# Own buffer for the pool weights, pool products ordered behind the sigmoid, two adding transfers in the output projection, and a bank of its own for the last half tile

## The chip, the cores and the metric

The kernel runs on one core of a Trainium2 chip. The metric is device time in microseconds (us) of one execution; lower is better. Engines are named as in the profile: PE is TensorE, DVE is VectorE, ACT is ScalarE, POOL is GpSimd, SP is SyncE, which here only issues transfers. Transfers are issued from a queue of SP, ACT or POOL.

## The reference

One decoder block for S = 512 tokens of width D = 1024, in float32. h = RMSNorm(x) is projected to q, k, v, a pool input u and two gates per output column. Differential attention in 8 heads and a multi-scale causal pool are gated, added, projected and added to x; a squared-ReLU MLP of width 4096 and a last norm follow.

```python
u_q, u_k, u_v, u_pool, u_gate = jnp.split(rmsnorm(x, g1) @ w_in, splits, axis=-1)
a = diff_attention(q, k, v, ...)         # per head: w = softmax_1 - lam * softmax_2, causal; o = w @ v, normed
p = multiscale_pool(u_pool, w_pool, pool_scale)   # per group g: d = windowed mean - u;  y = (d @ w_pool[g]) * scale
gates = jax.nn.sigmoid(u_gate)           # two gates per column
merged = gates[0] * a + gates[1] * p
x = x + merged @ w_out
x = x + relu(rmsnorm(x, g2) @ w_up) ** 2 @ w_down
return rmsnorm(x, gf)
```

There are 4 pool groups; group g serves heads 2g and 2g+1.

## The kernel before

Every product of float32 numbers is computed as three matmuls. A number is split into a high part of reduced precision (`fp32r`) and a low part, the rest; hi·hi, hi·lo and lo·hi are added up in PSUM. Names ending in `h` and `l` (`xh`, `xl`, `wh_`, `wl_`, `vh`, `vl`, `dh`, `dl`) are such parts; `wr_` is the raw weight as it was loaded.

A weight's parts are made in one of two ways. `split_w` casts the raw weight on ACT (L108) and subtracts on POOL, or on the engine that is passed, DVE (L109). With `"dma"`, `get_w` writes the high part on ACT (L116), writes its negative into the low part on ACT (L117), and lets a transfer issued on POOL add the weight out of memory a second time (L118).

The stages follow each other in this order. Up to about 55 us the kernel norms x and computes v for all heads. Up to about 305 us it works through heads 0 to 7: q and k of the head after, scores s, exp, p = the difference of the two softmaxes (L376), transposes t of p on PE (L380), their split (L382, L383), the product with v (PV, L388), and a norm over the head's output o. Between the heads stand 20 fillers, five for each pool group g: the projection and pooling of u (`pool`), and the gate projections ga and gp of its two heads (`gate`, L444). Behind the fifth, one sigmoid on ACT (L477) works on all four gates of the group, a table load (L478) follows, and `merge` runs for the two heads: the product pp of the pooled d and `w_pool` (L455 to L457), its eviction times the gate (L458), the sum with the head's gated output (L459), and its split (L460, L461). From about 305 to 360 us stands the output projection `po`, in two halves of columns, each with four weight blocks kk. Then come four quarters of the MLP, whose products are combined so that fewer are needed, up to 686 us, and the tail: the last product (L715) in three blocks of columns, their adds to x1 (L719), and the last norm and the stores (`square`, `finish`).

The program text is not the order of the work. A scheduler puts each engine's instructions into an order by its own estimate of when each can start, and every engine then works strictly in that order, waiting by semaphores where an operand or a buffer is not ready. `after(later, earlier)` tells this scheduler that one instruction has to come later than another, and creates no semaphore. Buffers are handed out by tag: a new tile of a tag waits until the readers of the tile that had the buffer are done. PSUM has eight banks; in the heads, `acc` gives bank 0, 1 and 2 in turn to the projections and to pp, in the order of the program text. So gp5, pp4, pp5, u3 and ga6 get banks 1, 2, 0, 1 and 2, and po0_0, which starts the output projection's banks over, gets bank 0, the one of pp6.

The pool weights `wpr` (L435) share a tag with other temporaries of the heads. They are cast and subtracted (L438, L439) into the third column of `wt_all`, which the transposes' parts use too.

Of the kernel before, what the change touches and what calls it, by code (L numbers as in the profile page):

```python
# [11 lines left out]
F32 = mybir.dt.float32  # L12
# [3 lines left out]
ALU = mybir.AluOpType  # L16
AX = mybir.AxisListType

P = 128
# [3 lines left out]
H = 8  # L23
NT = S // P
EPS = 1e-6
NCON = 313
LAM_INIT = 0.8 - 0.6 * math.exp(-0.3 * 0)
WINDOWS = (2, 4, 8, 16)
NEG = -3.0e38
# [23 lines left out]
def block_kernel(ctx, tc, xT, x_tok, gains, pos, consts, w_in, w_v, w_pool, w_out, w_up, w_dn, out):  # L53
    nc = tc.nc
    V, A, G, T = nc.vector, nc.scalar, nc.gpsimd, nc.tensor
# [3 lines left out]
    def after(later, earlier):  # L59
        tc.add_manual_dep(  # L60
            later.ins, earlier.ins.name,
            mybir.DependencyInfo(mybir.DependencyClass.NoSync, mybir.DependencyReason.DATA), reason="issue order",
        )

    ctx1 = ExitStack()
    cp = ctx.enter_context(tc.tile_pool(name="cp", bufs=1))
# [21 lines left out]
    def tmp(tag, name, shape=(P, S), dt=F32, bufs=2):  # L88
        return tp.tile(list(shape), dt, tag=tag, name=name, bufs=bufs)
# [22 lines left out]
    def get_w(src, name, eng=None):  # L112
        raw, hi, lo = load_w(src, name)
        if eng == "dma":

            A.copy(out=hi, in_=raw)  # L116
            A.mul(out=lo, in_=f(hi), mul=-1.0)  # L117
            G.dma_start(out=lo, in_=src, accum_op=ALU.add)  # L118
        else:
            split_w(raw, hi, lo, eng=eng)  # L120
        return hi, lo

    def mm3(acc, hi, lo, rh, rl):
# [7 lines left out]
            T.matmul(acc, lhsT=lo[:, c], rhs=rh[:, k, :], start=False, stop=k == NK - 1)  # L131


    con = cp.tile([P, NCON], F32, name="con")
    g1c, g2c, gfc, pscc = (con[:, 8 * i : 8 * i + 8] for i in range(4))
    wv0 = load_w(w_v[0, 0], "v0_0", 2, slice(0, 1))
    nc.sync.dma_start(out=g1c, in_=consts[:, 0:8])
    invc = con[:, 32:40]
    rcc = con[:, 40:56]
    lamv = con[:, 56:312].rearrange("p (a d) -> p a d", a=4)  # L140
    subc = con[:, 312:313]
    posi = cf.tile([P, NT], I32, name="posi")
    xh = B16(0, F32R, "xh")
    xl = B16(1, F32R, "xl")
# [11 lines left out]
        out=mask[:, 384:512], in_=mask[:, 384:512], pattern=[[-1, P]],  # L156
# [42 lines left out]
    for n in range(2):  # L199
        accs = [bank(4 * n + t, f"v{n}_{t}") for t in range(NT)]  # L200
        for kk in range(4):
            if n == 0:
                xprep(2 * kk)
            if n == 0 and kk == 0:
                raw, hi, lo = wv0
                nc.sync.dma_start(out=raw[:, 512:], in_=w_v[0, 0, :, 512:])
            else:
                raw, hi, lo = load_w(w_v[n, kk], f"v{n}_{kk}", 2 if n == 0 else 1)
            for k2 in range(2):
                if n == 0 and k2 == 1:  # L210
                    xprep(2 * kk + 1)
                sl = slice(k2 * 512, k2 * 512 + 512)
# [20 lines left out]
        for t in range(NT):  # L233
# [4 lines left out]
                out=vd[2], in0=av, scalar=rcol[:, t, 0:1], in1=vd[1],  # L238
                op0=ALU.mult, op1=ALU.subtract,
            )  # L240

    nc.sync.dma_start(out=con[:, 8:], in_=consts[:, 8:])
    nc.sync.dma_start(out=posi, in_=pos)

    lpr = tmp("pb", "lpr", (P, 2, 64), bufs=1)
# [13 lines left out]
    r_ = cf.tile(sh, F32, name="r_")  # L259
# [3 lines left out]
        out=r_, in0=posf.rearrange("p (t o) -> p t o", o=1).to_broadcast(sh),  # L263
        in1=invc.rearrange("p (o f) -> p o f", o=1).to_broadcast(sh), op=ALU.mult,
# [45 lines left out]
    acc = Rot((0, 1, 2))  # L310
# [98 lines left out]
    def pool(g):  # L409
        w = WINDOWS[g]  # L410
        a_ = proj(24 + g, f"u{g}", "dma")
        pad = tmp("u", f"u{g}", (P, 16 + S), bufs=1)
        G.memset(pad[:, :16], 0.0)
        u = pad[:, 16:]
        V.tensor_tensor(out=u, in0=a_, in1=rb, op=ALU.mult)
        bufs_ = [tmp("pa", f"pa{g}", (P, 16 + S), bufs=1), tmp("pb", f"pb{g}", (P, 16 + S), bufs=1)]
        for b_ in bufs_[:g]:
            G.memset(b_[:, :16], 0.0)
        cur, s_ = pad, 1
        n = 0  # L420
        while s_ < w:
            nxt = bufs_[n % 2]
            G.tensor_tensor(out=nxt[:, 16:], in0=cur[:, 16:], in1=cur[:, 16 - s_ : 16 + S - s_], op=ALU.add)
            cur, s_, n = nxt, 2 * s_, n + 1
        win = cur[:, 16:]
        d = bufs_[n % 2][:, 16:]
        V.scalar_tensor_tensor(out=d, in0=win, scalar=1.0 / w, in1=u, op0=ALU.mult, op1=ALU.subtract)
        V.tensor_tensor(out=d[:, :w], in0=win[:, :w], in1=rcc[:, :w], op=ALU.mult)
        V.tensor_tensor(out=d[:, :w], in0=d[:, :w], in1=u[:, :w], op=ALU.subtract)
        dh = tmp("dh", f"dh{g}", dt=F32R, bufs=1)  # L430
        dl = tmp("dl", f"dl{g}", dt=F32R, bufs=1)
        A.copy(out=dh, in_=d)
        V.tensor_tensor(out=dl, in0=d, in1=f(dh), op=ALU.subtract)
        wr = tmp("sq", f"wpr{g}", (P, 256))
        nc.sync.dma_start(out=wr, in_=w_pool[:, g, :])  # L435
        wph = wt_all[:, 0, 2, 0:256]
        wpl = wt_all[:, 1, 2, 0:256]
        A.copy(out=wph, in_=wr)  # L438
        V.tensor_tensor(out=wpl, in0=wr, in1=f(wph), op=ALU.subtract)  # L439
        return dh, dl, wph, wpl  # L440
# [2 lines left out]
        a_ = proj(m, name, "dma")  # L443
        V.tensor_tensor(out=dst, in0=a_, in1=rb, op=ALU.mult)  # L444

    def merge(h, a, sa, sp, dh, dl, wph, wpl):
        a, y = a
        if y is not None:
            V.scalar_tensor_tensor(out=a, in0=a, scalar=subc, in1=sa, op0=ALU.mult, op1=ALU.mult)
            V.tensor_tensor(out=a, in0=a, in1=y, op=ALU.mult)  # L450
        else:
            G.tensor_tensor(out=a, in0=a, in1=sa, op=ALU.mult)
        p_ = acc(f"pp{h}")
        c = slice((h % 2) * P, (h % 2) * P + P)
        T.matmul(p_, lhsT=wph[:, c], rhs=dh, start=True, stop=False)  # L455
        T.matmul(p_, lhsT=wph[:, c], rhs=dl, start=False, stop=False)
        T.matmul(p_, lhsT=wpl[:, c], rhs=dh, start=False, stop=True)  # L457
        V.scalar_tensor_tensor(out=sp, in0=p_, scalar=pscc[:, h : h + 1], in1=sp, op0=ALU.mult, op1=ALU.mult)  # L458
        V.tensor_tensor(out=a, in0=a, in1=sp, op=ALU.add)  # L459
        A.copy(out=mh[:, h, :], in_=a)  # L460
        V.tensor_tensor(out=ml[:, h, :], in0=a, in1=f(mh)[:, h, :], op=ALU.subtract)  # L461

    state = {}

    def filler_list():
        for g in range(4):
            def p_(g=g):
                state["gt", g] = tmp("g", f"g{g}", (P, 4, S), bufs=1)
                state["p", g] = pool(g)
            yield p_  # L470
            for i in range(4):
                h = 2 * g + i // 2
                def g_(g=g, i=i, h=h):
                    gate((28, 36)[i % 2] + h, ("ga", "gp")[i % 2] + str(h), state["gt", g][:, i])
                    if i == 3:
                        gt = state["gt", g]
                        sg = A.activation(out=gt, in_=gt, func=AF.Sigmoid)  # L477
                        after(A.preload_act_table_set(EXPLN), sg)  # L478
                yield g_

    fillers = list(filler_list())
    nf = 0
    outs = {}
    cur = qk(0)
    for h in range(H):
        outs[h] = attn(h, *cur)
        cur = qk(h + 1) if h < H - 1 else None
        while nf < LAG[h]:
            fillers[nf]()
            nf += 1  # L490
            if nf % 5 == 0:
                g = nf // 5 - 1
                gt = state["gt", g]
                for i in range(2):
                    merge(2 * g + i, outs[2 * g + i], gt[:, 2 * i], gt[:, 2 * i + 1], *state["p", g])

    ctx1.close()
    bk = ctx.enter_context(tc.tile_pool(name="bk", bufs=1, reuse_waits="tile"))
    acc = Rot(tuple(range(8)))

    x1 = big.tile([P, NT, D], F32, tag="s0", name="x1")
# [42 lines left out]

    po = [acc(f"po0_{t}") for t in range(NT)]
    for kk in range(4):
        w = get_w(w_out[0, kk], f"o0_{kk}", V if kk % 2 else None)
        for k in (2 * kk, 2 * kk + 1):
            for t in range(NT):
                mm_rows(po[t], t, k, w, k == 0, k == NK - 1)  # L550
# [7 lines left out]
    for t in range(NT):  # L558
        a_ = acc(f"po1_{t}")
# [60 lines left out]
    def down(q):  # L620
# [49 lines left out]
        w = parts(x_, "t3", V)  # L670
# [30 lines left out]
        if not last:  # L701
            to_x1(product(A22, w4, "m4", onto=m7), 1, 0)
            return
        for t in (0, 1):
            square(t, 1, yr[:, 1])
        fin = [finish(t, 1) for t in (0, 1)]

        cols = ((0, 0, 512), (1, 0, 256), (1, 256, 512))
        for a, c0, c1 in cols:
            for p in range(4):  # L710
                hi, lo = w4[p // 2]
                sl, tsl = slice((p % 2) * 512 + c0, (p % 2) * 512 + c1), slice(a * P, a * P + P)
                zh, zl = zfh[:, A22, p, tsl], zfl[:, A22, p, tsl]
                for l_, r_ in ((zh, hi), (zh, lo), (zl, hi)):
                    T.matmul(m7[a][:, c0:c1], lhsT=l_, rhs=r_[:, sl], start=False, stop=p == 3 and r_ is hi and l_ is zl,  # L715
                             skip_group_check=True)
            t = 2 + a
            xs = x1[:, t, c0:c1]
            evict = V.tensor_tensor(out=xs, in0=m7[a][:, c0:c1], in1=xs, op=ALU.add)  # L719
            if a == 0:  # L720
                for i in fin:
                    after(i, evict)

            to = 6 if c1 == 256 else 0
            A.activation(out=yr[:, a, c0:c1], in_=xs, func=AF.Square, accum_out=st[:, t, to : to + 1])
            if c1 == 256:
                V.tensor_tensor(out=st[:, t, 1:2], in0=st[:, t, 1:2], in1=st[:, t, 6:7], op=ALU.add)
                row_early(t, 1)
            else:
                finish(t, 0, a == 1)  # L730
# [72 lines left out]
```

## Time and profile before

| | |
|---|---|
| runs | 697.95, 695.3, 697.5 us; median 697.5 |
| the profiled execution | 697.38 us, its span 695.6 us |
| PE busy | 679.3 us, 98% of the span |
| DVE, ACT, POOL busy | 476.4, 420.0, 161.2 us |
| DMA | 100.88 MB, 145 GB/s in the mean |

The profile is one execution. Its span runs from the first instruction to the last; the time of the execution holds 1.8 us more. A row of the timeline gives the start, the duration, the engine, the line, the operation, output and inputs; the bracket behind it tells how long the engine stood idle before, and what it waited for last. "SPq" and "POOLq" are the queues of transfers.

### The profile page before, as it was taken

To read this page: it belongs to the slowest core of one execution; us is meant where nothing else is said; L and a number is where in the kernel's file an instruction comes from. 1 tells how busy PE (TensorE), PEld (TensorE's weight loads), DVE (VectorE), ACT (ScalarE), POOL (GpSimd) and SP (SyncE) were. 2 spreads that over 40 slices of the span, in tenths; PEclk is the share of its full clock that TensorE was granted. 3 is DMA by queue.
4 is the path that set the end of the run, shared out by engine and by line. 5 is a ranking of instruction groups with operands and counts; after the bars stand their busy time and mean duration, and the time that the engine had idled before them with its cause. 6 is when DMAs were issued, how large, how long until landed. Compare 5 with 4: busy or idle time off the path is not lost.

```text
span 695.6 us, 8855 instructions
## 1 busy us (share of the span) xinstructions
PE 679.3 (98%) x3158; PEld 564.3 (81%) x3158; DVE 476.4 (68%) x834; ACT 420.0 (60%) x683; POOL 161.2 (23%) x151
## 2 busy tenths in 40 slices
PE   8999999999999999999999999999999999999995
PEld 7788878888888887787888888888888888888884
DVE  6953977789788875965385675555765567645785
ACT  7554487977986689674356644455434554355544
POOL 6101634264345525532300010000210011000100
PEclk9999999999999999999999999999999999999998
DMA  7534574426436365345943269823797249952523
GB/s 268 165 115 116 133 150 120 103 63 157 125 88 151 99 152 121 91 163 201 246 128 118 91 107 288 231 100 91 179 247 209 90 92 209 248 177 91 95 57 122
DMA packets 30140, 100.88 MB, mean 145 GB/s; under 512 B 3600, under 2 KB 4240, under 8 KB 30096
## 3 DMA queue, kind: packets, MB, share of 16 engines
q1 hardware_dynamic: 22464, 72.79, 30.0%
q0 software_dynamic: 7488, 27.27, 23.0%
q8 instruction: 25, 0.41, 0.2%
q10 hardware_dynamic: 144, 0.26, 0.1%
q14 instruction: 19, 0.16, 0.1%
HBM read 98.20 MB, written 2.10 MB: 144 GB/s over the span
## 4 chain that ended last, share of the span: by engine, by line
PE 78%; DVE 10%; ACT 6%; issue 2%; DMA 2%; POOL 1%; SPq 0%; DVEq 0%; ACTq 0%; POOLq 0%
PE pu L127 8%; PE pu L128 8%; PE pu L131 8%; PE m L652 7%; PE m L653 7%; PE m L651 7%; PE po L536 2%; PE po L537 2%; PE po L538 2%; DVE p L376 2%; PE q L127 2%; PE k L127 2%; PE k L128 2%; PE q L128 2%; PE q L131 2%
## 5 line engine op out<-in xcount | busy, mean ns | idle before, releaser
L127 PE MATMUL pu<-x1gh,wh_up 128*128 128x512 f32 (+1 forms) x272 | 101.0, 377 | 0.2 <-ACT x1gh L571 0.2
L128 PE MATMUL pu<-x1gl,wh_up 128*128 128x512 f32 (+1 forms) x272 | 101.1, 377 | 0.0
L641 POOL DMA_DIRECT2D wr_b<-w_dn x32 | 27.7, 927 | 299.7 <-DVE wl_t L109 228.5
L109 DVE TENSOR_TENSOR wl_up<-wr_up,wh_up 128x1024 fp32r<-128x1024 f32 x32 | 39.2, 1225 | 41.8 <-ACT wh_up L108 30.3
L131 PE MATMUL pu<-x1gh,wl_up 128*128 128x512 f32 (+1 forms) x272 | 64.0, 377 | 0.0
L108 ACT CAST wh_up<-wr_up 128x1024 fp32r<-128x1024 f32 x32 | 33.7, 1053 | 44.4 <-PE m L653 20.0
L127 PEld LDWEIGHTS pu<-x1gh,wh_up 128*128 128x128 f32 x272 | 51.0, 188 | 9.8 <-ACT x1gh L571 0.5
L128 PEld LDWEIGHTS pu<-x1gl,wh_up 128*128 128x128 f32 x272 | 51.2, 188 | 9.6 <-DVE x1gl L572 0.2
L131 PEld LDWEIGHTS pu<-x1gh,wl_up 128*128 128x128 f32 x272 | 49.2, 188 | 9.3
L108 ACT CAST wh_t<-wr_b 128x1024 fp32r<-128x1024 f32 x32 | 33.6, 1053 | 38.1 <-PE m L653 24.6
L109 DVE TENSOR_TENSOR wl_t<-wr_b,wh_t 128x1024 fp32r<-128x1024 f32 x32 | 38.9, 1224 | 22.8 <-ACT wh_t L108 13.2
L604 DVE TENSOR_TENSOR zfl<-zr,zfh 128x512 fp32r<-128x512 f32 (+1 forms) x32 | 34.9, 1091 | 26.8 <-ACT zfh L603 26.8
L651 PE MATMUL m<-wh_t,zfh 128*128 128x512 f32 x120 | 46.7, 389 | 0.0
L652 PE MATMUL m<-wl_t,zfh 128*128 128x512 f32 x120 | 46.7, 389 | 0.0
L653 PE MATMUL m<-wh_t,zfl 128*128 128x512 f32 x120 | 46.7, 389 | 0.0
L371 ACT ACTIVATE p<-p,st 128x128 f32<-128x128 f32 (+3 forms) x64 | 35.8, 560 | 17.6 <-DVE st L367 17.1
L603 ACT CAST zfh<-zr 128x512 fp32r<-128x512 f32 (+1 forms) x32 | 30.2, 944 | 23.6 <-DVE zr L601 16.6
L652 PE MATMUL m<-wl_b,zfh 128*128 128x512 f32 x96 | 37.3, 389 | 0.0
L653 PE MATMUL m<-wh_b,zfl 128*128 128x512 f32 x96 | 37.3, 389 | 0.0
L651 PE MATMUL m<-wh_b,zfh 128*128 128x512 f32 x96 | 37.2, 389 | 0.0
L376 DVE SCALAR_TENSOR_TENSOR p<-p,st 128x128 f32<-128x128 f32 (+3 forms) x32 | 28.9, 902 | 8.0 <-ACT p L375 8.0
L109 DVE TENSOR_TENSOR wl_b<-wr_b,wh_b 128x1024 fp32r<-128x1024 f32 x16 | 19.6, 1224 | 18.4 <-PE pu L131 9.9
(266 smaller groups left out, 1794.4 us busy)
## 6 DMA issues: line engine op xcount, KB each, us to landing
wr_b<-w_dn SPq DMA_DIRECT2D x32, 512.0 KB, 3.8
wr_up<-w_up SPq DMA_DIRECT2D x32, 512.0 KB, 6.2
wr_b<-w_dn POOLq DMA_DIRECT2D x32, 512.0 KB, 5.9
wr_q<-w_in SPq DMA_DIRECT2D x8, 512.0 KB, 3.2
wr_k<-w_in SPq DMA_DIRECT2D x8, 512.0 KB, 3.3
wr_ga<-w_in SPq DMA_DIRECT2D x8, 512.0 KB, 3.2
wr_gp<-w_in SPq DMA_DIRECT2D x8, 512.0 KB, 3.4
wl_ga<-w_in POOLq DMA_DIRECT2D x8, 512.0 KB, 5.7
```

Source lines behind the costliest of these rows:

```text
L108: ins = A.copy(out=hi[:, sl], in_=raw[:, sl])
L109: (eng or G).tensor_tensor(out=lo[:, sl], in0=raw[:, sl], in1=f(hi)[:, sl], op=ALU.subtract)
L127: T.matmul(acc, lhsT=hi[:, c], rhs=rh[:, k, :], start=k == 0, stop=False)
L128: T.matmul(acc, lhsT=hi[:, c], rhs=rl[:, k, :], start=False, stop=False)
L131: T.matmul(acc, lhsT=lo[:, c], rhs=rh[:, k, :], start=False, stop=k == NK - 1)
L371: A.activation(out=pr[:, c, :N], in_=pr[:, c, :N], func=AF.Exp, scale=-1.0, bias=st[:, c : c + 1], accum_out=st[:, 2 + c : 3 + c])
L376: V.scalar_tensor_tensor(out=pr[:, 0, :N], in0=pr[:, 0, :N], scalar=st[:, 4:5], in1=pr[:, 1, :N], op0=ALU.mult, op1=ALU.add)
L603: A.copy(out=zfh[:, sl, p, :], in_=F[:, sl])
L604: V.tensor_tensor(out=zfl[:, sl, p, :], in0=F[:, sl], in1=f(zfh)[:, sl, p, :], op=ALU.subtract)
L651: T.matmul(pa[a], lhsT=zh, rhs=hi[:, sl], start=p == 0 and onto is None, stop=False, skip_group_check=True)
L652: T.matmul(pa[a], lhsT=zh, rhs=lo[:, sl], start=False, stop=False, skip_group_check=True)
L653: T.matmul(pa[a], lhsT=zl, rhs=hi[:, sl], start=False, stop=p == 3 and stop, skip_group_check=True)
```

## The change

1. The constants tile `con` is cut to 57 columns. The four lambda vectors get a temporary tile with its own transfer, so there is one more transfer in the opening.
2. `wpr` gets a buffer of its own. Its load, its cast and its subtraction may so come before other temporaries are done.
3. For heads 4 to 7 the first product of `merge` is ordered after its group's sigmoid.
4. Blocks 0 and 2 of the first half of `w_out` are split by `"dma"`: no POOL subtraction, but one more pass on ACT and an adding transfer each. Blocks 1 and 3 stay on DVE, and the second half is unchanged.
5. In the tail, the last block of columns (256 to 511 of the fourth token tile) is computed in a bank of its own, `m4b`. The sum that lay in its old bank is added to x1 beforehand, by one more DVE instruction, and the second and third block are ordered behind the one ahead of each.

```diff
-    con = cp.tile([P, NCON], F32, name="con")
+    con = cp.tile([P, 57], F32, name="con")
...
-    nc.sync.dma_start(out=con[:, 8:], in_=consts[:, 8:])
+    lamv = tmp("pa", "lamv", (P, 4, 64), bufs=1)
+    nc.sync.dma_start(out=con[:, 8:], in_=consts[:, 8:57])
+    nc.sync.dma_start(out=lamv.rearrange("p a d -> p (a d)"), in_=consts[:, 57:])
...
-        wr = tmp("sq", f"wpr{g}", (P, 256))
+        wr = tmp("wpr", f"wpr{g}", (P, 256), bufs=1)
...
-    def merge(h, a, sa, sp, dh, dl, wph, wpl):
+    def merge(h, sg, a, sa, sp, dh, dl, wph, wpl):
...
-        T.matmul(p_, lhsT=wph[:, c], rhs=dh, start=True, stop=False)
+        first_ = T.matmul(p_, lhsT=wph[:, c], rhs=dh, start=True, stop=False)
+        if h > 3:
+            after(first_, sg)
...
-        w = get_w(w_out[0, kk], f"o0_{kk}", V if kk % 2 else None)
+        w = get_w(w_out[0, kk], f"o0_{kk}", V if kk % 2 else "dma")
...
+        xs = x1[:, 3, 256:512]
+        V.tensor_tensor(out=xs, in0=xs, in1=m7[1][:, 256:], op=ALU.add)
...
         for a, c0, c1 in cols:
+            a_ = acc("m4b")[:, :256] if c0 else m7[a][:, c0:c1]
...
-                    T.matmul(m7[a][:, c0:c1], lhsT=l_, rhs=r_[:, sl], start=False, stop=p == 3 and r_ is hi and l_ is zl,
+                    m = T.matmul(a_, lhsT=l_, rhs=r_[:, sl], start=c0 > 0 and p == 0 and l_ is zh and r_ is hi, stop=p == 3 and r_ is hi and l_ is zl,
                              skip_group_check=True)
+                    if a and p == 0 and l_ is zh and r_ is hi:
+                        after(m, end)
+            end = m
...
-            evict = V.tensor_tensor(out=xs, in0=m7[a][:, c0:c1], in1=xs, op=ALU.add)
+            evict = V.tensor_tensor(out=xs, in0=a_, in1=xs, op=ALU.add)
```

Lines behind these edits move by a few: L455 to L457 become L455, L458 and L459, the eviction L458 becomes L460, and the products L536 to L538 of po become L539 to L541.

The order changes at three places. On PE, around the pool products of heads 4 and 5 (the row of `ss5` is a piece of a head's norm, `t6_2` are transposes of head 6), before:

```order
L401 MATMUL ss5_2239<-sql5_2235,onesr_88 128x512
L131 MATMUL gp5_2611<-xh_81,wl_gp5_2607 128x512
L455 MATMUL pp4_2640<-dh2_2091,wt_531 128x512
L456 MATMUL pp4_2640<-dl2_2092,wt_531 128x512
L457 MATMUL pp4_2640<-dh2_2091,wt_531 128x512
L455 MATMUL pp5_2649<-dh2_2091,wt_531 128x512
L456 MATMUL pp5_2649<-dl2_2092,wt_531 128x512
L457 MATMUL pp5_2649<-dh2_2091,wt_531 128x512
L380 MATMUL t6_2_2458<-ident_83,p6_2_2442 128x128 x3
L127 MATMUL u3_2781<-xh_81,wh_u3_2776 128x512
```

and after:

```order
L401 MATMUL ss5_2241<-sql5_2237,onesr_88 128x512
L130 MATMUL gp5_2613<-xh_81,wl_gp5_2609 128x512
L380 MATMUL t6_2_2460<-ident_83,p6_2_2444 128x128 x3
L126 MATMUL u3_2783<-xh_81,wh_u3_2778 128x512
L455 MATMUL pp4_2642<-dh2_2093,wt_533 128x512
L458 MATMUL pp4_2642<-dl2_2094,wt_533 128x512
L459 MATMUL pp4_2642<-dh2_2093,wt_533 128x512
L455 MATMUL pp5_2651<-dh2_2093,wt_533 128x512
L458 MATMUL pp5_2651<-dl2_2094,wt_533 128x512
L459 MATMUL pp5_2651<-dh2_2093,wt_533 128x512
L127 MATMUL u3_2783<-xl_82,wh_u3_2778 128x512
```

pp4 and pp5 have moved behind the transposes and the first product of u3.

On PE in the first half of the output projection (`vh` and `vl` stand for the merged, split rows), around the pool products of heads 6 and 7, before:

```order
L537 MATMUL po0_3_2994<-wl_o0_2_3058,vh_107 128x512
L538 MATMUL po0_3_2994<-wh_o0_2_3057,vl_108 128x512
L400 MATMUL ss7_2764<-sqh7_2758,onesr_88 128x512
L401 MATMUL ss7_2764<-sql7_2760,onesr_88 128x512
L455 MATMUL pp6_2963<-dh3_2820,wt_531 128x512
L456 MATMUL pp6_2963<-dl3_2821,wt_531 128x512
L455 MATMUL pp7_2973<-dh3_2820,wt_531 128x512
L456 MATMUL pp7_2973<-dl3_2821,wt_531 128x512
L457 MATMUL pp6_2963<-dh3_2820,wt_531 128x512
L457 MATMUL pp7_2973<-dh3_2820,wt_531 128x512
L536 MATMUL po0_0_2991<-wh_o0_0_2997,vh_107 128x512
```

After, they stand between two rows of po0_3 and po0_2:

```order
L539 MATMUL po0_3_2996<-wh_o0_1_3030,vh_107 128x512
L540 MATMUL po0_3_2996<-wl_o0_1_3031,vh_107 128x512
L455 MATMUL pp6_2965<-dh3_2822,wt_533 128x512
L458 MATMUL pp6_2965<-dl3_2823,wt_533 128x512
L459 MATMUL pp6_2965<-dh3_2822,wt_533 128x512
L455 MATMUL pp7_2975<-dh3_2822,wt_533 128x512
L458 MATMUL pp7_2975<-dl3_2823,wt_533 128x512
L459 MATMUL pp7_2975<-dh3_2822,wt_533 128x512
L539 MATMUL po0_2_2995<-wh_o0_0_2999,vh_107 128x512
L540 MATMUL po0_2_2995<-wl_o0_0_3000,vh_107 128x512
L541 MATMUL po0_2_2995<-wh_o0_0_2999,vl_108 128x512
L539 MATMUL po0_2_2995<-wh_o0_0_2999,vh_107 128x512
```

and further on come the first reader of `wl_o0_2`, the norm of head 7 and the first product of po0_0:

```order
L541 MATMUL po0_2_2995<-wh_o0_1_3030,vl_108 128x512
L541 MATMUL po0_3_2996<-wh_o0_1_3030,vl_108 128x512
L539 MATMUL po0_2_2995<-wh_o0_2_3060,vh_107 128x512
L540 MATMUL po0_2_2995<-wl_o0_2_3061,vh_107 128x512
L541 MATMUL po0_2_2995<-wh_o0_2_3060,vl_108 128x512
L539 MATMUL po0_3_2996<-wh_o0_2_3060,vh_107 128x512
L400 MATMUL ss7_2766<-sqh7_2760,onesr_88 128x512
L540 MATMUL po0_3_2996<-wl_o0_2_3061,vh_107 128x512
L541 MATMUL po0_3_2996<-wh_o0_2_3060,vl_108 128x512
L539 MATMUL po0_2_2995<-wh_o0_2_3060,vh_107 128x512
L539 MATMUL po0_0_2993<-wh_o0_0_2999,vh_107 128x512
```

The pool products stand earlier, and between pp7 and po0_0 there are now products of po0_2 and po0_3.

On POOL, around block 0 of `w_out` (L423 are steps of the pooling, L452 a gating product, L397 and L398 pieces of a norm), before:

```order
L118 DMA wl_gp7_2930<-w_in 128x1024
L423 TENSOR_TENSOR pb3_2810<-pa3_2809 128x512
L109 TENSOR_TENSOR wl_o0_0_2998<-wr_o0_0_2995,wh_o0_0_2997 128x1024
L452 TENSOR_TENSOR o5_2231<-o5_2231,g2_2045 128x512
L397 TENSOR_TENSOR sqo6_2505<-o6_2500 128x512
L398 TENSOR_TENSOR sql6_2504<-sqo6_2505,sqh6_2502 128x512
L109 TENSOR_TENSOR wl_o0_2_3058<-wr_o0_2_3055,wh_o0_2_3057 128x1024
```

and after:

```order
L117 DMA wl_gp7_2932<-w_in 128x1024
L423 TENSOR_TENSOR pb3_2812<-pa3_2811 128x512
L452 TENSOR_TENSOR o5_2233<-o5_2233,g2_2047 128x512
L117 DMA wl_o0_0_3000<-w_out 128x1024
L397 TENSOR_TENSOR sqo6_2507<-o6_2502 128x512
L398 TENSOR_TENSOR sql6_2506<-sqo6_2507,sqh6_2504 128x512
L117 DMA wl_o0_2_3061<-w_out 128x1024
L452 TENSOR_TENSOR o6_2502<-o6_2502,g3_2775 128x512
```

The two subtractions are gone; the transfer for block 0 is issued behind the gating product of head 5, the one for block 2 ahead of that of head 6.

More of the change, by code (lines that the diff above doesn't have):

```diff
@@ L25 @@
 EPS = 1e-6
-NCON = 313
 LAM_INIT = 0.8 - 0.6 * math.exp(-0.3 * 0)
@@ L139, in block_kernel @@
     rcc = con[:, 40:56]
-    lamv = con[:, 56:312].rearrange("p (a d) -> p a d", a=4)
-    subc = con[:, 312:313]
+    subc = con[:, 56:57]
     posi = cf.tile([P, NT], I32, name="posi")
@@ L478, in g_ @@
                         after(A.preload_act_table_set(EXPLN), sg)
+                        state["sg", g] = sg
                 yield g_
@@ L494, in block_kernel @@
                 for i in range(2):
-                    merge(2 * g + i, outs[2 * g + i], gt[:, 2 * i], gt[:, 2 * i + 1], *state["p", g])
+                    merge(2 * g + i, state["sg", g], outs[2 * g + i], gt[:, 2 * i], gt[:, 2 * i + 1], *state["p", g])
     ctx1.close()
@@ L777 @@
         + [np.broadcast_to(v.astype(np.float32), (P, v.size)) for v in (
-            inv, np.float32(1) / np.arange(1, 17, dtype=np.float32), lam4.reshape(-1))]
-        + [col(a(subln_g)[0])], axis=1)
+            inv, np.float32(1) / np.arange(1, 17, dtype=np.float32))]
+        + [col(a(subln_g)[0]), np.broadcast_to(lam4.reshape(-1), (P, lam4.size))], axis=1)
     arrays = {
```

## The prediction

> **What bounds the kernel now.** I read the page first, then PE's waits, then busy time in windows, then the timeline around each wait.
>
> ```profile
> span 695.6 us, 8855 instructions
> PE 679.3 (98%) x3158; PEld 564.3 (81%) x3158; DVE 476.4 (68%) x834; ACT 420.0 (60%) x683; POOL 161.2 (23%) x151
> ```
>
> TensorE is busy for 679.3 of 695.6 us, and the change neither adds nor removes a product. So only the 16.3 us in which PE stands can be won, and a new stall costs its full length. The view of PE's waits (engine, line, what it waited for: us, times, longest) names what it stands for:
>
> ```profile
> PE v L217 <- ACT xh L175: 1.9, 1, 1.9
> PE ga L127 <- DVE g L458: 1.4, 1, 1.4
> PE t L380 <- DVE p L376: 1.2, 1, 1.2
> PE m L715 <- DVE x L719: 1.1, 1, 1.1
> PE pp L455 <- ACT wt L438: 1.1, 1, 1.1
> PE po L536 <- DVE g L458: 0.6, 1, 0.6
> ```
>
> The first is in the opening, which keeps its products. The other five are single events and belong to the places that the change touches. The windows (stretch, length, busy time by engine, PE clock, DMA share, GB/s) say whether time won there reaches the end:
>
> ```profile
> 300.00:320.00 20.00, 18.30 (x85) 14.63 (x84) 10.08 (x16) 13.15 (x17) 3.70 (x2) 1.00 0.53 191
> 320.00:340.00 20.00, 20.00 (x90) 16.55 (x89) 11.38 (x22) 9.11 (x15) 8.87 (x6) 1.00 0.80 246
> 400.00:680.00 280.00, 280.00 (x1237) 231.86 (x1236) 178.61 (x221) 138.55 (x164) 24.16 (x28) 1.00 0.60 156
> ```
>
> From 320 us on PE does not stand again until the tail, and the granted clock is 1.00: a microsecond won before 320 us should arrive whole at the end.
>
> **Part 1, pool products behind the sigmoid (pp4, pp5).**
>
> ```profile
> 266.42 0.39 PE L131 MATMUL gp<-xh,wl_gp 128*128 128x512 f32 x1
> 266.65 0.40 PE L455 MATMUL pp<-dh,wt 128*128 128x512 f32 x1
> 267.37 0.68 DVE L444 TENSOR_TENSOR g<-gp,rb 128x512 f32<-128x512 f32 x1
> 268.29 0.48 PE L127 MATMUL u<-xh,wh_u 128*128 128x512 f32 x1
> 272.04 1.28 ACT L477 ACT_TABLE_LOAD   x1
> 273.34 1.92 ACT L477 ACTIVATE g<-g 128x2048 f32<-128x2048 f32 x1
> 275.29 1.41 DVE L458 SCALAR_TENSOR_TENSOR g<-pp,con,g 128x512 f32<-128x512 f32 x2 [3.03 <-ACT g L477]
> 276.09 0.50 PE L127 MATMUL ga<-xh,wh_ga 128*128 128x512 f32 x1 [1.35 <-DVE g L458]
> 276.56 0.48 ACT L382 CAST wt<-t 128x384 fp32r<-128x384 f32 x1
> ```
>
> ga6 takes the bank of pp4, which the eviction L458 frees, which waits for the sigmoid: that is the 1.35 us. The edit orders instructions and adds no semaphore. In the new order pp4 and pp5 move behind three transposes and one product of u, still far ahead of where the sigmoid starts, so the sigmoid still sets ga's start. u3 shares its bank with gp5. Before, six pool products, from 266.65 on at 0.23 each, hid gp5's eviction, which ends at 268.05. After, PE reaches u about 267.0 and stands some 1.1 us: a new wait, on the same L444. It delays PE ahead of the old wait, which shrinks by as much; the two together come to the old 1.35. On ACT the cast of t_2 (0.48), which stood behind the table load, now stands ahead of it. ACT runs without a gap up to 272.04, so sigmoid and ga come 0.48 us later. Cost 0.5. Bounds: were ga's wait gone and only u's left, 1.35 - 1.1 = a gain of 0.25; were both full, with the cast, a cost of 1.1 + 0.48 = 1.6. I take 0.5, since the rows give all its terms.
>
> **Part 2, low parts by adding transfers (blocks 0 and 2 of w_out's first half).**
>
> ```profile
> 283.15 4.23 DVE L376 SCALAR_TENSOR_TENSOR p<-p,st 128x128 f32<-128x128 f32 x1
> 283.30 1.59 POOL L423 TENSOR_TENSOR pb<-pa 128x512 f32<-128x512 f32 x1
> 284.55 2.67 POOL L109 TENSOR_TENSOR wl_o<-wr_o,wh_o 128x1024 fp32r<-128x1024 f32 x1
> 287.52 0.30 PE L380 MATMUL t<-ident,p 128*128 128x128 f32 x1 [1.25 <-DVE p L376]
> ```
>
> A 128x128 operation on DVE lasts 4.23 us, and ends just as POOL's two instructions do: DVE is held for as long as POOL works. By the Trainium skill, "SBUF — State Buffer", section "SBUF: two separate sides", VectorE and GpSimd share a port pair as an exclusive lock; this row fits it. With POOL's subtraction gone, DVE should be free when L423 ends at 284.89, and p is written well before 286.27, where PE began to stand. The gain is 1.25; bounds 0 (another POOL instruction takes its place) and 1.25. I take 1.2.
>
> What replaces it: a pass on ACT and an adding transfer from POOL's queue, for each of two weights. The same pair exists for ga:
>
> ```profile
> 301.23 1.05 ACT L108 CAST wh_o<-wr_o 128x1024 fp32r<-128x1024 f32 x1
> L117 ACT ACTIVATE wl_ga<-wh_ga x8: 1042/1060/1072, 70.2 to 271.0; 128x1024 fp32r<-128x1024 f32 x8
> L118 POOL DMA_DIRECT2D wl_ga<-w_in x8: 858/877/887, 71.5 to 272.3; - x8
> DMA to landing us min/median/max: 5.3/5.6/7.3
> DMA to landing us min/median/max: 8.0/11.9/15.1
> 305.51 0.39 PE L536 MATMUL po<-wh_o,vh 128*128 128x512 f32 x1
> ```
>
> (The first landing row is for L118; the second is for the four POOL loads of w_down at 332 us, the most crowded of this kernel.) For block 2 the cast ends at 302.3, one more cast and the new pass (1.06) end about 304.0, so the transfer lands at 309.3 to 311.3. On PE its first reader stands 43 matmuls behind the start of po (90 in the 20.00 us from 320 on, 0.22 each; with two changes of shape I take 9.0): 305.5 + 9.0 - 0.7 won by then = 313.8. Covered by 2.5 us. If x_tok's four loads, issued at 305.7, stretched it to 11.9, it would land at 315.9 and stall PE 2.1; to 15.1, at 319.1 and 5.3. I take 0.2. Block 0 is cast some 20 us before use. The two ACT passes (2.1 us) fall where ACT has gaps (13.15 of 20 us from 300 on); were they on the path, the cost would be 2.1.
>
> Against this edit speaks the same page of the Trainium skill, section "A bandwidth-pool intuition that's wrong (but worth ruling out)": a DMA issued by GpSimd takes 620 ns alone and 3100 ns while VectorE holds that port, since its descriptors can't be written. This trace shows no such spread: L118's eight issues for ga differ by 29 ns. By the rule the transfer would land 2.5 us later (an estimate from that page), 313.8 at worst, and the sum would be the same by either.
>
> **Part 3, own buffer for the pool weights, and pp6, pp7.**
>
> ```profile
> 309.24 0.68 SPq L435 DMA_DIRECT2D wpr<-w_pool  x1
> 316.90 0.40 ACT L438 CAST wt<-wpr 128x256 fp32r<-128x256 f32 x1 [4.84 <-DMA wpr<-w_pool]
> 317.36 0.50 PE L455 MATMUL pp<-dh,wt 128*128 128x512 f32 x1 [1.09 <-ACT wt L438]
> 318.82 1.41 DVE L458 SCALAR_TENSOR_TENSOR g<-pp,con,g 128x512 f32<-128x512 f32 x2 [1.06 <-PE pp L457]
> 319.63 0.50 PE L536 MATMUL po<-wh_o,vh 128*128 128x512 f32 x1 [0.61 <-DVE g L458]
> ```
>
> The last pool weights are loaded late behind x_tok, land after 7.6 us, and PE waits 1.09 for their cast; then po_0 waits 0.61 for pp6's eviction, whose bank it takes. After, load and cast are done some 40 us earlier, and 21 products (4.8 us) stand between pp7 and po_0 against an eviction of 1.41. Both go: 1.70. Bounds 0 (the wait turns into block 2's) and 1.70; I take 1.7, the transfer's own risk being counted above. The earlier loads, casts (0.40) and subtractions keep their number; the split second constants load adds one issue in the opening, behind work of v, at nothing; were that cover gone, 0.7 for the issue.
>
> **Part 4, the tail.**
>
> ```profile
> 686.41 0.42 DVE L719 TENSOR_TENSOR x<-m,x 128x256 f32<-128x256 f32 x1
> 686.88 0.39 PE L715 MATMUL m<-wh_t,zfh 128*128 128x256 f32 x1 [1.14 <-DVE x L719]
> 688.30 0.28 PE L715 MATMUL m<-wh_t,zfl 128*128 128x256 f32 x1
> 688.62 0.42 DVE L719 TENSOR_TENSOR x<-m,x 128x256 f32<-128x256 f32 x1
> 690.93 0.72 ACT L742 ACTIVATE x<-x,st 128x512 f32<-128x512 f32 x1 [0.48 <-DVE st L530]
> ```
>
> The last twelve products wait 1.14 for the eviction of the other half of their bank. In a bank of their own they do not, and PE ends 1.1 to 1.4 us sooner. But then the last add stands ahead of the third tile's norm chain, which DVE and ACT did during that wait; it costs the end a 0.74 us scaling and parts of 0.2. Gain 0.75; bounds 0.3 and 1.2. The new add (0.42 by the same rows) comes about 669 us, where PE is saturated: nothing, or 0.42 if DVE were late with weights.
>
> **Sum** against the profiled execution (697.38 us; its span is 695.6, and 1.8 lie around it): +0.5 - 1.2 + 0.2 - 1.7 - 0.75 = -2.95, 694.4. That execution is 0.12 below the median, 697.5, so this is 0.44% less. Rows elsewhere between 200 and 300 us also change places on DVE and ACT; PE has few gaps there, and I price this at nothing, within 1 either way.
>
> **Rivals.** (1) *All five waits go*, the pool products really hide the sigmoid and u does not stand: 1.35 + 1.25 + 1.09 + 0.61 + 1.14 = 5.4, so 692.0. For: each edit names one of them. Against: u's bank and the unmoved sigmoid. (2) *Slower: block 2's transfer lands late.* It decides when the stall passes the gains, 3.15 us: a landing over 13 us after issue. At 15.1 the stall is 5.3 and the time 699.6. For: the loads around 306 us. Against: 5.3 to 7.3 in all twenty issues so far; at 11.9 the time is 696.3. (3) *A wait moves on*: the changed order makes DVE late for another transpose, or the tail's chain keeps its length, and about 1.2 of the gain is lost: 695.7. For: DVE is the partner in four of the five waits.
>
> **Numbers.** Forecast 0.50, rival 1 0.20, rival 2 0.12, rival 3 0.18. A difference under 0.5% (3.5 us, so 694.0 to 701.0) is no change for such a measurement. Faster: most of rival 1 and two fifths of the forecast, 0.39. Slower by over 0.5%: only rival 2 past 16.7 us of landing, or a stall in what I priced at nothing, 0.08. Same 0.53. The range takes in rival 1 less a little scatter and most of rival 2: 691.8 to 698.0.
>
> **What would show it.** In the profile after: u's first product waiting some 1.1 us for L444 and ga for less than 1.35; the 128x128 row of L376 below 2 us; no wait at pp6, pp7 or po_0; the first reader of block 2's low part not waiting; PE's last product about 3 us earlier against the start than its own 688.30. I am wrong if PE waits at that reader, or if u does not wait at all.

## The result, and the profile after

The changed kernel took 692.63 us (median of 4 runs, 692.48 to 692.81) against 697.65 of the kernel before (4 runs, 695.3 to 697.95): ratio 0.9935, interval 0.9918 to 0.9951. A second measurement (e9) gave 692.79 against 697.22: 0.9940, 0.9927 to 0.9952. So it is faster by 0.6%. The forecast of 694.4 had the sign and the range right, and some 2 us too little gain. It gave 0.53 to a change below 0.5% and 0.39 to a larger gain; the gain is 0.65%, and its interval begins at 0.49%.

The page of the profile after, its first lines, and the view of PE's waits:

```profile
span 691.0 us, 8851 instructions
PE 678.2 (98%) x3158; PEld 564.6 (82%) x3158; DVE 471.2 (68%) x835; ACT 422.5 (61%) x685; POOL 158.6 (23%) x151
```

```profile
PE v L215 <- ACT xh L173: 1.5, 1, 1.5
PE t L380 <- DVE p L376: 1.3, 1, 1.3
PE warm L159 <- POOL onesr L148: 1.1, 1, 1.1
PE u L126 <- DVE g L444: 0.5, 1, 0.5
PE s L365 <- DVE st L367: 0.4, 1, 0.4
PE pu L126 <- ACT x1gh L574: 0.2, 1, 0.2
```

All five waits that the prediction listed for the touched places are gone. The t wait of 1.3 is not the old one: it stands at 167 us, and the old one stood at 287. The windows from 260 us on:

```profile
260.00:280.00 20.00, 19.54 (x93) 16.05 (x92) 12.73 (x35) 18.49 (x32) 10.60 (x9) 1.00 0.46 100
280.00:300.00 20.00, 20.00 (x99) 16.80 (x98) 17.19 (x38) 16.44 (x34) 9.44 (x9) 1.00 0.55 136
300.00:320.00 20.00, 20.00 (x94) 16.59 (x94) 10.89 (x16) 12.13 (x15) 2.54 (x3) 1.00 0.56 181
```

PE stands for 0.46 us in these 60 us. The timeline after, at the places of parts 1, 2, 3 and 4:

```profile
164.52 0.85 POOL L117 DMA_DIRECT2D wl_gp<-w_in  x1
164.80 2.03 DVE L376 SCALAR_TENSOR_TENSOR p<-p,st 128x128 f32<-128x128 f32 x1
165.12 1.54 POOL L323 TENSOR_TENSOR swq<-swq,tab 128x512 f32<-128x512 f32 x1
166.97 0.30 PE L380 MATMUL t<-ident,p 128*128 128x128 f32 x1 [1.35 <-DVE p L376]
...
268.00 0.69 DVE L444 TENSOR_TENSOR g<-gp,rb 128x512 f32<-128x512 f32 x1 [0.63 <-PE gp L130]
268.75 0.50 PE L126 MATMUL u<-xh,wh_u 128*128 128x512 f32 x1 [0.46 <-DVE g L444]
273.62 1.92 ACT L479 ACTIVATE g<-g 128x2048 f32<-128x2048 f32 x1
276.70 0.40 PE L126 MATMUL ga<-xh,wh_ga 128*128 128x512 f32 x1
...
283.36 2.30 DVE L406 SCALAR_TENSOR_TENSOR o<-o,con,y 128x512 f32<-128x512 f32 x1
283.51 1.59 POOL L423 TENSOR_TENSOR pb<-pa 128x512 f32<-128x512 f32 x1
285.66 0.33 DVE L376 SCALAR_TENSOR_TENSOR p<-p,st 128x128 f32<-128x128 f32 x1
...
300.42 0.88 POOL L117 DMA_DIRECT2D wl_o<-w_out  x1 [5.38 <-ACT wl_o L116]
308.60 0.39 PE L455 MATMUL pp<-dh,wt 128*128 128x512 f32 x1
313.21 0.39 PE L540 MATMUL po<-wl_o,vh 128*128 128x512 f32 x1
...
681.79 0.28 PE L722 MATMUL m4b<-wh_t,zfh 128*128 128x256 f32 x1
683.11 0.28 PE L722 MATMUL m4b<-wh_t,zfl 128*128 128x256 f32 x1
686.83 0.40 ACTq L755 DMA_DIRECT2D out<-x  x1
```

Near 165 us a 128x128 operation on DVE lasts 2.03 us, until POOL's L323 is done, and PE waits: this wait is new. Before, the same operation was over when L323 began:

```profile
163.56 0.35 DVE L376 SCALAR_TENSOR_TENSOR p<-p,st 128x128 f32<-128x128 f32 x1
164.42 1.60 POOL L323 TENSOR_TENSOR swq<-swq,tab 128x512 f32<-128x512 f32 x1
```

At 268 us u waits 0.46 where 1.1 was expected, and ga starts without a wait. Near 284 us POOL holds DVE's L406 in place of L376, for L423 alone, and the 128x128 operation takes 0.33. pp6 does not wait; the first reader of block 2's low part (313.21) finds it there, its transfer having been issued at 300.42 and landed within 6.6 us:

```profile
DMA to landing us min/median/max: 5.6/6.1/6.6
```

(the landings of the two `wl_o` transfers). The last store is issued at 686.83 in place of 691.68.

To compare places, I count from `pt`, the first product after v, up to which PE's order is the same in all these kernels: it starts at 52.78 before and at 52.23 after. Differences to before, in us, of the start of a k product near 197 us, of ga6, of the first product of the MLP (pu) and of PE's last product, each from pt (positive is later; in kernels with the order behind the sigmoid ga6 stands two short products, 0.24 us, further back in PE's order):

| kernel | k (197) | ga6 | pu | last product |
|---|---|---|---|---|
| after | +1.63 | +1.16 | -3.21 | -4.64 |
| e9 after, again | +1.57 | +1.08 | -3.27 | -4.69 |
| e1 tail alone | +0.06 | +0.09 | -0.22 | -1.64 |
| e2 constants alone | +0.13 | +0.16 | +0.07 | +0.06 |
| e3 adding transfers alone | +0.03 | +0.06 | -2.54 | -2.55 |
| e4 behind the sigmoid alone | +0.08 | +0.42 | -1.75 | -1.76 |
| e5 own weight buffer alone | +1.60 | +0.43 | -1.75 | -1.75 |
| e6 after, not behind the sigmoid | +1.56 | +0.38 | -3.60 | -5.02 |
| e7 after, POOL subtractions | +1.61 | +1.10 | -2.51 | -3.92 |
| e8 after, shared weight buffer | +0.11 | +0.46 | -1.59 | -3.00 |
| e10 own buffer for group 3 alone | +0.09 | +0.09 | -3.90 | -5.32 |
| e11 e10 behind the sigmoid | +0.10 | +0.47 | -3.81 | -5.22 |
| e12 e10 with early eviction | +0.18 | -0.52 | -2.89 | -4.30 |

Each row is one trace; the changed kernel has two, which agree within 0.08. The intervals of the times of e6 to e12 all overlap that of the changed kernel, so what sets these kernels apart is read from the table.

### The profile page after: what moved, and what is told of

Read it like the earlier page. It is cut to its first block, busy times and chain, and to the rows that moved or that the text cites. A ratio compares the mean times of both kernels' runs of the same rounds, so it can differ in the third digit from the quotient of the medians.

```text
span 691.0 us, 8851 instructions
## 1 busy us (share of the span) xinstructions
PE 678.2 (98%) x3158; PEld 564.6 (82%) x3158; DVE 471.2 (68%) x835; ACT 422.5 (61%) x685; POOL 158.6 (23%) x151
## 4 chain that ended last, share of the span: by engine, by line
PE 90%; DVE 5%; ACT 2%; issue 1%; DMA 1%; POOL 0%; SPq 0%; ACTq 0%; POOLq 0%
PE pu L126 8%; PE pu L127 8%; PE pu L130 8%; PE m L654 7%; PE m L655 7%; PE m L656 7%; PE v L215 2%; PE po L539 2%; PE v L217 2%; PE gp L126 2%; PE gp L127 2%; PE gp L130 2%; PE po L540 2%; PE po L541 2%; PE v L216 2%; PE q L126 2%
## 5 line engine op out<-in xcount | busy, mean ns | idle before, releaser
L367 DVE CUSTOM_DVE_ANT_0 p<-s,mask 128x128 f32<-128x128 f32 (+3 forms) x64 | 29.8, 482 | 2.0 <-PE s L366 2.0
```

What stands on the lines that cost most here:

```text
L367: V.tensor_tensor_reduce(out=pr[:, c, :N], in0=s_[:, :N], in1=mask[:, S - N :], scale=-0.125, scalar=-NEG, op0=ALU.add, op1=ALU.min, accum ...
```

## The experiments

**e1, the tail alone.**

```diff
+            a_ = acc("m4b")[:, :256] if c0 else m7[a][:, c0:c1]
```

> The kernel before with the tail's edit alone (own bank for the last block of columns). Theory A (each wait removed from PE is worth its listed idle time plus about 0.27 us in which PE empties and fills again): PE's last product starts 1.4 us earlier than 688.30, the last store is issued about 1.0 us earlier than 691.68, time 1.0 us below before. Rival B (a wait is worth its listed idle time and nothing more; what the whole change won beyond that came from elsewhere): last product 1.14 earlier, end 0.75 earlier.

Measured: 696.36 us, ratio 0.9990 (0.9981 to 0.9999), which is 0.1 to 1.3 us below before and fits both theories. In the trace they part: from pu to the last product e1 is 1.42 us faster, and up to pp6 the order is that of before. The last store is issued at 690.83, which from pu on is 1.08 earlier. The wait had 1.14 listed: theory A. The rows of before show the other 0.27 at the wait for the pool weights, whose first product starts at 317.36:

```profile
315.87 0.40 PE L401 MATMUL ss<-sql,onesr 128*128 128x512 f32 x1
...
317.69 0.40 PE L456 MATMUL pp<-dl,wt 128*128 128x512 f32 x1
```

In a dense stretch two products start 0.23 apart though each row is 0.40 long. Here the starts are 1.49 and 0.33 apart: 1.36 lost, while the list says 1.09. The list counts from the end of the last row, which is 0.17 behind the point at which the next product would have started in a dense stretch, and the product behind the wait is followed 0.10 later than usual.

**e2, the constants' split alone.**

```diff
+    lamv = tmp("pa", "lamv", (P, 4, 64), bufs=1)
+    nc.sync.dma_start(out=con[:, 8:], in_=consts[:, 8:57])
```

> The kernel before with the constants' transfer split alone; the order of PE stays the same throughout. Theory A: the opening's gain of the whole change (first product of v 0.37 us earlier, the wait of 0.20 for xl gone, k of head 2 at 159.5 in place of 160.2) belongs to this edit: time 0.5 to 0.7 us below before. Rival B: the opening's start scatters from run to run, whatever the constants: v starts within 0.1 of 6.78 and the time is the same.

Measured: 697.53, ratio 1.0010 (1.0001 to 1.0018), so no faster; nothing in the table changes by more than 0.16. That is against theory A. Rival B holds in that the opening scatters and the time does not follow it, but not in its sign: v starts at 5.62 here, not near 6.78. The pace scatters too. The first products of e1 and then of after, with the same operands:

```profile
5.61 0.80 PE L217 MATMUL v<-wh_v,xh 128*128 128x512 f32 x1 [0.69 <-ACT xh L175]
6.21 0.63 PE L218 MATMUL v<-wl_v,xh 128*128 128x512 f32 x1
```

```profile
6.41 0.50 PE L215 MATMUL v<-wh_v,xh 128*128 128x512 f32 x1 [1.49 <-ACT xh L173]
6.75 0.39 PE L216 MATMUL v<-wl_v,xh 128*128 128x512 f32 x1
```

In e1 the products that follow start 0.43 apart, in after 0.23. The profile gives a granted clock of 1.00 for both stretches, and nothing in the rows says why. pt starts anywhere from 51.82 to 53.87 us in the ten profiles with the split of the constants, and from 52.12 to 53.23 in the four without it. So the 0.55 that the first comparison shows there is not counted as a gain of the change.

**e3, the adding transfers alone.**

```diff
-        w = get_w(w_out[0, kk], f"o0_{kk}", V if kk % 2 else None)
+        w = get_w(w_out[0, kk], f"o0_{kk}", V if kk % 2 else "dma")
```

> The kernel before with the two adding transfers alone. Theory A: the 128x128 row of L376 near 283 us falls from 4.23 to below 2 us, PE's wait of 1.25 goes and is worth 1.5; the first reader of block 2's low part does not wait; pp6 still waits 1.09 for its weights: time 1.5 us below before. Rival B: the transfers' landing or the two more ACT passes take it back: PE waits at the reader or for an ACT cast, 0 to 0.5 below.

Measured: 694.87, ratio 0.9972 (0.9961 to 0.9983), so 2.2 below before where 1.5 was expected. The 128x128 row of L376 falls from 4.23 to 1.91, since only L423 holds it now, the t wait is gone, and po starts 1.38 earlier from pt: theory A, with one thing beyond it. The wait at pp6 went too, without the pool weights' own buffer: their load landed in 6.7 us, and their cast ended 0.05 before PE's product, with no wait listed. Why the load landed sooner than in the 7.6 us of before is not shown.

```profile
282.55 1.91 DVE L376 SCALAR_TENSOR_TENSOR p<-p,st 128x128 f32<-128x128 f32 x1
282.70 1.60 POOL L423 TENSOR_TENSOR pb<-pa 128x512 f32<-128x512 f32 x1
...
306.94 0.55 SPq L435 DMA_DIRECT2D wpr<-w_pool  x1
313.70 0.41 ACT L438 CAST wt<-wpr 128x256 fp32r<-128x256 f32 x1 [3.93 <-DMA wpr<-w_pool]
314.16 0.50 PE L455 MATMUL pp<-dh,wt 128*128 128x512 f32 x1
```

**e4, behind the sigmoid alone.**

```diff
+        if h > 3:
+            after(first_, sg)
```

> The kernel before with pool products ordered behind the sigmoid alone. Theory A (as predicted: u waits 1.1 for gp5's eviction, ga still waits for the sigmoid, which is 0.3 to 0.5 later; the gain at this place in the whole change came from PE arriving 1.1 late, not from this edit): 0.3 to 0.8 us above before, with two waits in the view of PE. Rival B: the edit itself removes ga's wait: 0.5 to 0.9 below, no wait at ga.

Measured: 695.40, ratio 0.9977 (0.9967 to 0.9986). At the place itself theory A holds: u waits, ga still waits a little, and ga6 is 0.42 later, of which 0.24 are the two products ahead of it. Yet the kernel is faster, against theory A, and not as rival B has it. In the other order POOL's subtraction L109 (2.40 us from 287.61) holds a 128x256 operation of DVE some 3 us further on, and the transposes behind it wait 0.83 in place of 1.25; and the pool weights again land in time.

```profile
268.28 0.50 PE L127 MATMUL u<-xh,wh_u 128*128 128x512 f32 x1 [0.95 <-DVE g L444]
276.62 0.51 PE L127 MATMUL ga<-xh,wh_ga 128*128 128x512 f32 x1 [0.21 <-DVE g L460]
290.43 0.41 PE L380 MATMUL t<-ident,p 128*128 128x128 f32 x2 [0.83 <-DVE p L376]
```

**e5, the constants' split and the own weight buffer.**

```diff
-        wr = tmp("sq", f"wpr{g}", (P, 256))
+        wr = tmp("wpr", f"wpr{g}", (P, 256), bufs=1)
```

> The kernel before with the constants' split and the pool weights' own buffer alone. Theory A: this edit changes the order from 120 us on and so carries two things: the waits at pp6 and po0_0 go (1.09 + 0.61 listed, worth 2.2 to 2.4), and the new wait of 1.35 near 167 us, where L376 is held by POOL's L323, appears here; it makes PE late and so shrinks ga's wait of 1.35 to near nothing, so that it costs almost nothing at the end: time 2.5 to 3.0 us below before, with the opening's 0.5. Rival B: the wait near 167 us costs its full length: 1.0 to 1.5 below. Rival C: it belongs to another edit and is absent here.

Measured: 695.65, ratio 0.9973 (0.9962 to 0.9984), so 1.5 below before where 2.5 to 3.0 were expected. The new wait appears here (1.41 near 168 us): rival C falls. It makes PE 1.60 late, and 1.17 of that is given back by ga6, which no longer waits: between theory A and rival B. In the same order s waits 0.46 and t 0.56 near 290 us.

**e6, e7, e8: the change less one part.** e6 drops the order behind the sigmoid, e7 the adding transfers, e8 the own buffer.

```diff
-            after(first_, sg)
```

> The changed kernel without the order behind the sigmoid. Theory A: pp4 and pp5 hide gp5's eviction again, so u's wait of 0.46 (worth 0.7) goes; PE then reaches ga about when the sigmoid's eviction ends, so ga waits 0 to 0.7: time 0 to 0.7 us below the changed kernel. Rival B: the order is what freed ga: a wait of 1.0 or more at ga, 0.5 or more above the changed kernel.

Measured: 692.69, ratio 0.9928 (0.9909 to 0.9947); the last product is 0.38 earlier than in after, and neither u nor ga waits. Theory A by the trace: in this change the order behind the sigmoid wins nothing.

```diff
-        w = get_w(w_out[0, kk], f"o0_{kk}", V if kk % 2 else "dma")
+        w = get_w(w_out[0, kk], f"o0_{kk}", V if kk % 2 else None)
```

> The changed kernel with POOL's two subtractions back in place of the adding transfers; PE's order is the same throughout. Theory A: DVE is held near 283 us again by POOL's subtraction (an operation of 4 us or so), PE waits about 1.3 there: time 1.3 to 1.6 us above the changed kernel. Rival B: in the new order another operation stands there and the hold costs nothing: same time.

Measured: 693.88, ratio 0.9943 (0.9925 to 0.9960); the last product is 0.72 later than in after. DVE is held again, but now it is L427, 5 us further on, and the transposes wait 0.56. That is half of what theory A expected, for the order had changed:

```profile
287.94 2.40 POOL L108 TENSOR_TENSOR wl_o<-wr_o,wh_o 128x1024 fp32r<-128x1024 f32 x1
288.42 2.47 DVE L427 SCALAR_TENSOR_TENSOR pa<-pb,u 128x512 f32<-128x512 f32 x1
291.43 0.41 PE L380 MATMUL t<-ident,p 128*128 128x128 f32 x2 [0.56 <-DVE p L376]
```

```diff
-        wr = tmp("wpr", f"wpr{g}", (P, 256), bufs=1)
+        wr = tmp("sq", f"wpr{g}", (P, 256))
```

> The changed kernel with the pool weights back in the shared buffer (the constants' split kept). Theory A: the wait near 167 us is gone, pp6's wait for the weights and po0_0's for the eviction are back (worth 2.2 to 2.4 together), and at 268 to 276 us u and ga wait some 1.1 more than in the changed kernel, since PE arrives earlier: time 2.2 to 2.6 us above the changed kernel. Rival B: the wait near 167 us cost its full length, so its absence pays: 0.5 to 1.0 above.

Measured: 694.18, ratio 0.9957 (0.9939 to 0.9974); the last product is 1.64 later than in after, between the two expectations. The wait near 167 is gone. The weights' wait (0.83) and po_0's (0.61) are back, and u waits 0.97.

**e9, the changed kernel again; e10 to e12 on the same chip.**

> The changed kernel once more, for the same chip and runs as the next three. Theory A (the opening's 0.55 of the first comparison is scatter of the chip, the rest is the change): the distance between the start of stage two (first transpose product pt) and PE's last product is 630.3 us as in its first profile, within 0.3, with the same waits, the 1.35 near 167 us among them; the first products of v may run at another pace. Rival B: the waits scatter too.

Measured: 692.79, ratio 0.9940; every entry of the table within 0.08 of the first profile, the wait near 167 at 1.37: theory A. (From pt to the last product it is 630.83 us, in the first profile 630.88; the 630.3 of the expectation was misreckoned.)

e10 gives the own buffer to the last group only, the one that waited, and drops the order behind the sigmoid; e11 has that order.

```diff
-        wr = tmp("sq", f"wpr{g}", (P, 256))
+        wr = tmp("wpr", f"wpr{g}", (P, 256), bufs=1) if g == 3 else tmp("sq", f"wpr{g}", (P, 256))
```

> Constants' split, adding transfers, own bank in the tail, and the own pool weight buffer for the last group alone (the other three groups share as before), no order behind the sigmoid. Up to the waits at 276 us the order is that of before. Theory A (the wait near 167 us comes from the earlier loads and casts of the first groups; PE's lateness from it shortened the wait at ga): no wait near 167, ga waits 1.35 again, no wait at t near 287, at pp6 and po0_0: from pt to PE's last product about 5.3 us less than before, 0.6 less than the changed kernel; time 0.4 to 0.8 below the changed kernel. Rival B (the wait near 167 cost its full length): ga does not wait 1.35 in this order either and 1.6 us are won.

> As the one before, with pool products ordered behind the sigmoid. Theory A (with PE on time, this order trades ga's wait for one at u): u waits 0.9 to 1.1, ga 0.2 to 0.4; time within 0.5 us of the one before, rather above it. Rival B: ga's wait goes and 0.8 or more is won.

Measured: e10 692.16, ratio 0.9929 (0.9916 to 0.9941); e11 691.89, 0.9929 (0.9915 to 0.9942). The last product of e10 is 5.32 earlier than before, as expected. PE's longest waits of e10 outside the opening, and then the two of e11 that differ:

```profile
PE ga L126 <- DVE g L458: 1.4, 1, 1.4
...
PE s L365 <- DVE st L367: 0.4, 1, 0.4
```

```profile
PE u L126 <- DVE g L444: 1.0, 1, 1.0
PE ga L126 <- DVE g L460: 0.3, 1, 0.3
```

With the first groups' loads where they were, the wait near 167 is gone and ga's 1.4 is back: the one had been hiding the other. Behind the sigmoid, 1.4 turns into 1.0 and 0.3. Theory A in both. Both kernels are below the changed one in the same runs, by 0.6 and 0.9 us of median, with intervals that overlap its own; the traces show 0.6 and 0.5. All five executions of e10 lie below all five of e9 (at most 692.50 against at least 692.68); those of e11 go up to 693.27.

e12 takes ga's wait away at its source, by evicting pp4 and pp5 without the gate.

```diff
+        if h in (4, 5):
+            e_ = tmp("pa" if h == 4 else "pb", f"ppe{h}", (P, 16 + S), bufs=1)[:, 16:]
+            V.tensor_scalar(out=e_, in0=p_, scalar1=pscc[:, h : h + 1], scalar2=None, op0=ALU.mult)
+            V.tensor_tensor(out=sp, in0=e_, in1=sp, op=ALU.mult)
```

> As the one without the order behind the sigmoid, but pp4 and pp5 are evicted to SBUF by a DVE operation of their own as soon as they are done, and multiplied by the gate behind the sigmoid: two more 128x512 operations on DVE. Theory A (ga waits for its bank, which the sigmoid holds back through the eviction): ga's wait of 1.35 goes and is worth 1.6 us against the one without; 690.5 or so, 1.5 to 2.2 below the changed kernel. Rival B: DVE or ACT is what PE waits for next there, a wait of 0.5 or more at t or s of head 6 or 7 takes its place, and 0 to 1 is won.

Measured: 693.82, ratio 0.9949 (0.9936 to 0.9961), slower than e10. ga does not wait: it starts at 275.19, while the sigmoid is at work until 276.26, so the bank was its reason. Two things take the gain back. PE comes to u 1.11 later than in e10, for which no wait above 0.2 us is listed there and whose cause is open, so ga6 is only 0.61 earlier. Behind ga6 1.63 is lost: DVE's 128x128 operation meets POOL's L423, and PE waits at t. Rival B.

```profile
285.00 1.57 POOL L423 TENSOR_TENSOR pb<-pa 128x512 f32<-128x512 f32 x1
285.14 1.59 DVE L376 SCALAR_TENSOR_TENSOR p<-p,st 128x128 f32<-128x128 f32 x1
286.88 0.30 PE L380 MATMUL t<-ident,p 128*128 128x128 f32 x1 [1.01 <-DVE p L376]
```

## Why the prediction was right, and where it was short

From pt to the issue of the last store the change won 4.30 us (638.90 to 634.60); the prediction's sum was 2.95. Parts 2 to 4 were set 1.77 too low; the first two rows below together cost 0.92 for a forecast of 0.5, and that these two come so near is luck, since neither was right by itself. The terms, with what the two first traces show (ga6's two products taken off; po starts at 304.17 in place of 305.51, from pt 0.79 earlier):

| | predicted | measured |
|---|---|---|
| wait near 167 us | not seen | +1.63 at k |
| part 1, sigmoid | +0.5 | -0.71 (k to ga6) |
| part 2, transfers | -1.2 + 0.2 | -1.71 (ga6 to po) |
| part 3, pool weights | -1.7 | -2.42 (po to pu) |
| part 4, tail | -0.75 | -1.09 (pu to the last store's issue) |

- **Part 1** was right in kind: by e4, e10 and e11 the edit turns ga's wait into one at u and costs 0.1 to 0.2. The sigmoid came later about as forecast (from pt 0.42 in e4, and 0.36 in e11 against e10, for 0.48). Still 0.5 was too much, since the two short products that stood behind ga6 (0.24) now run ahead of it. The -0.71 of the trace is not its doing: without it (e5, e6) 1.17 and 1.18 come back there.
- **The step that failed** is "I price this at nothing, within 1 either way", on the rows that change places between 200 and 300 us. The order changes from 120 us on, and not only at the three places named ahead of the prediction, by the earlier loads and casts of the first three groups' pool weights (e5, e8, e10), and near 165 us, ahead of the stretch that was priced, a hold of DVE by POOL arises of the very kind that part 2 removes: PE is 1.63 later behind it. At the end it cost little, because PE then came late to a wait set by the sigmoid: by e10 against e6 0.30 us, by e11 against after 0.58. Rival 3 named it in kind.
- **Parts 2, 3 and 4** were right in mechanism and too small. The listed idle time of a wait (1.25, 1.70 in two, 1.14) is less than it costs; 0.27 more for each (e1) gives 1.52, 2.24 and 1.41 on PE. The 0.2 for a late transfer was not needed. 0.2 us in each of parts 2 and 3 stays unexplained; that of part 3 lies at the first sixteen transposes `h2T`, near 350 us, from whose start to the next product it is 2.20 before and 2.00 after.
- **Part 4** lost less to the tail than was set down: 1.42 on PE gave 1.08 at the end, not 0.75.
- **Rival 1**, all five waits go, said 692.0, nearer to the 692.63 than the forecast. The five did go, but not by its mechanism: the pool products do not hide the sigmoid, u stands 0.46, and with PE on time (e10, e11) a wait at ga or u is there again. That its number is near is luck: what the waits cost beyond the listed time about makes up for the new wait and for what the tail loses.
- **Block 2's transfer**, the rival of the slower side, landed 6 us before its reader. The Trainium skill, "SBUF — State Buffer", section "A bandwidth-pool intuition that's wrong (but worth ruling out)", would have such a transfer wait while VectorE holds the shared port; the two issues took 0.88 us each and landed within 6.6: no run here shows that wait.
- **The single edits do not add up.** On PE's last product e1, e3, e4 and e5 win 1.64, 2.55, 1.76 and 1.75, together 7.70, and the whole 4.64. pp6's wait of 1.09 hung on a transfer that landed in 7.6 us, or in 6.7 and 6.8 with e3 and e4, and vanished in e3, e4 and e5: three edits were each paid for the same wait.

## What to carry to other kernels

On PE, always busy here, a wait cost some 0.3 us more than the idle time that the profile lists (1.36 for 1.09, 1.42 for 1.14): count from start to start of the instructions, less the usual distance. An edit that lets a scheduler place loads and casts earlier is an edit of the whole order behind them; compare the orders for the places where one engine holds another, and apply it only where the wait was. A wait that disappears may have been hidden by lateness from another one, so an edit is judged by adding it alone and by removing it alone.

## What was not expected of the hardware

The operations on DVE that POOL held had started, by their rows, ahead of the POOL instruction that held them: 164.80 against 165.12, 283.36 against 283.51 (2.30 us for an operation that takes 0.74), and in before 283.15 against 283.30. Each time POOL was then issuing a transfer, from 164.52 for 0.85 us, from 282.90 for 0.88 and from 282.69 for 0.88. The Trainium skill, "SBUF — State Buffer", section "SBUF: two separate sides", gives the shared port, for an operation of VectorE with two inputs in SBUF, to whichever starts first; by their recorded starts these rows differ. That the issue of the transfer counts as the first does not explain it, by these rows of before:

```profile
213.42 0.89 POOL L118 DMA_DIRECT2D wl_gp<-w_in  x1 [4.87 <-ACT wl_gp L117]
213.60 0.74 DVE L406 SCALAR_TENSOR_TENSOR o<-o,con,y 128x512 f32<-128x512 f32 x1
214.03 1.34 POOL L423 TENSOR_TENSOR pa<-u 128x512 f32<-128x512 f32 x1
```

Here DVE starts within an issue too and takes its usual 0.74. It starts 0.43 ahead of POOL's operation, and the held ones started 0.15 to 0.32 ahead. Whether that distance decides, or the recorded starts are not exact, no run separated.
